# One 512-column matmul for both halves of the activations in 81 weight-stationary projections

## The chip, the cores and the metric

The kernel runs on one core of one Trainium2 chip. The metric is the time of one execution on the device in microseconds (us). Of the engines, TensorE (PE; PEld is its loading of weights) multiplies, VectorE (DVE) and ScalarE (ACT) work on elements, GpSimd (POOL) does small work, and SyncE (SP) starts the transfers of the weights.

## The reference

Two blocks of two layers each run on one sequence of 256 tokens with 1024 features, in float32.

```python
def first_block(...):
    for i in range(DEPTH):                      # 2
        h = h + mixer(rmsnorm(h, norm_mix[i]))  # 0: retention, 1: band attention
        h = h + ffn(rmsnorm(h, norm_ffn[i]))    # 0: SwiGLU of 2816, 1: 8 experts, top 2
        h = h + per_layer_embedding(...)
    return rmsnorm(h, norm_final)

def second_block(x, ...):
    for l in range(DEPTH):                      # 2
        h = rms_norm(x, norm_mix[l])
        x = x + hybrid_mixer(h, ...)            # stick-breaking, top-k attention, HGRN2
        h2 = rms_norm(x, norm_mlp[l])
        x = x + jnp.square(jax.nn.relu(h2 @ w_up[l])) @ w_down[l]
    return x
```

Each `@` with a weight is one of the projections below. The SwiGLU's gate and up weights, the MLP's up weights, the queries and keys of retention and of attention, and the `hq`, `hf`, `sq`, `sk` columns of `w_in` are those that the change touches.

## The kernel before

Every product with a weight is made of three matmuls (`mm3`, L337): both operands are split into a high part and a low part (`whi`, `wlo` for weights, `xth`, `xtl` for activations), and hi*hi, hi*lo and lo*hi are added in one PSUM bank of 128 partitions x 512 float32. The weights come from HBM in chunks (`wraw`) and are split in the kernel, `whi` on ACT (L288) and `wlo` on DVE (L289), into 5 buffers that run ahead of PE. So PE, ACT and DVE all work on every weight, and each engine does its instructions in the order in which a scheduler wrote them down when the kernel was built.

There are two kinds of projection. In `lin_tok` (and `down`) the activations are the stationary operand and the weights pass as 512 columns. In `lin_feat` (L422) it is the other way: the stationary is a 128x128 piece of weights and the 256 tokens pass, so its output has features on the partitions and tokens along the row. A call of `lin_feat` makes 256 features in two halves `f`, each with 8 steps `k` over the 1024 features of the input, three matmuls of 256 columns per step. Both halves go to one bank, side by side, and the caller reads the 512 columns straight from PSUM with its own first operation (L580 and L582 in retention, L707 in the dense layer, L793 in attention, L1356 and L1358 for the stick-breaking keys, L1421 and L1431 for HGRN2, L1524 in the MLP).

`lin_feat` is called 81 times: 8 in retention, 21 in the dense layer, 8 in attention, and in each of the two layers of the second block 4 for HGRN2, 3 for stick-breaking and 15 in the MLP. The banks that it takes turns through (`banks(mm=...)`) are three in the dense layer and the MLP ("012") and two elsewhere ("01" or "45").

In the MLP each step j makes one `lin_feat` and then the `down` product of step j-1: 24 matmuls of 512 columns that add up in four banks of their own (`acc`). Between the two stand the square of the rectified projection (L1524, L1525) and its split (`hh`, `hl`). In the hybrid layer PE gets the `lin_feat` matmuls of stick-breaking while DVE is busy with `select_keys` (L1310 to L1318), which finds the 64 best keys of each query.

## Time and profile before

| | |
|---|---|
| time, median of 3 runs | 2466.2 us (2464.65 to 2468.09) |
| the profiled execution | 2464.32 us |
| its span, first to last instruction | 2462.5 us |
| granted TensorE clock, mean | 0.997 |

The profiled execution is one more run of the same program, and the rows below are from it. Its time stands 1.9 us under the median, and 1.8 us of it lie around the span.

### The profile page before, as it was taken

What the parts mean: (1) busy time and instruction counts of PE and PEld (TensorE: products, weight loads), DVE (VectorE), ACT (ScalarE), POOL (GpSimd) and SP (SyncE); (2) the same over time, 40 slices, a digit from 0 to 9 for tenths busy, and PEclk for the clock granted to TensorE, in tenths of its full rate; (3) what the DMA queues carried; (4) which work ended last, traced back from release to release, by engine and by line L of the source; (5) the groups of instructions that cost most, each with busy time, mean ns of one, the idle gap of its engine ahead of it and who ended that gap; (6) DMA issues with size and microseconds to landing.
All of it is one profiled execution on the core that took longest, in us unless ns stands there. A gap on an engine that the chain in (4) does not pass through costs nothing. (4 is left out here: it accounts for less than half of the span.)

```text
span 2462.5 us, 35589 instructions
## 1 busy us (share of the span) xinstructions
PE 2402.0 (98%) x13060; PEld 1987.3 (81%) x13060; DVE 1880.3 (76%) x2964; ACT 1564.7 (64%) x2607; POOL 61.3 (2%) x105
## 2 busy tenths in 40 slices
PE   8999999999999999998999999899999999999999
PEld 6978998887876787865788875698779989877998
DVE  6757557658989889888989899878676567867655
ACT  6446556657887777777777788645745554575554
POOL 0000000000000000000000000101000000100000
PEclk9999999999999999999999999999999999999999
DMA  7445555557989998999899989534255554434553
GB/s 283 171 165 215 190 187 187 192 234 279 368 319 393 346 370 338 362 351 352 336 366 353 362 349 378 152 130 172 105 177 209 188 173 133 172 113 173 192 193 111
DMA packets 88391, 605.70 MB, mean 246 GB/s; under 512 B 10480, under 2 KB 12144, under 8 KB 17296
## 3 DMA queue, kind: packets, MB, share of 16 engines
q1 hardware_dynamic: 85792, 593.91, 65.0%
q0 software_dynamic: 2416, 9.44, 1.7%
q8 instruction: 104, 1.70, 0.3%
q14 instruction: 79, 0.65, 0.1%
HBM read 602.26 MB, written 1.05 MB: 245 GB/s over the span
## 5 line engine op out<-in xcount | busy, mean ns | idle before, releaser
L289 DVE TENSOR_TENSOR wlo<-wraw,whi 128x512 fp32r<-128x512 f32 (+1 forms) x1656 | 1379.9, 875 | 366.9 <-ACT whi L288 355.2
L288 ACT ACTIVATE whi<-wraw 128x512 fp32r<-128x512 f32 (+1 forms) x1656 | 1201.6, 775 | 436.7 <-PE mm L340 203.6
L341 PE MATMUL mm<-xth,wlo 128*128 128x256 f32 x1296 | 363.5, 280 | 1.5 <-DVE wlo L289 1.5
L339 PE MATMUL mm<-xth,whi 128*128 128x256 f32 x1296 | 364.9, 282 | 0.0
L340 PE MATMUL mm<-xtl,whi 128*128 128x256 f32 x1296 | 364.3, 281 | 0.0
L341 PEld LDWEIGHTS mm<-xth,wlo 128*128 128x128 f32 x1296 | 246.7, 190 | 2.4 <-DVE wlo L289 1.7
L341 PE MATMUL acc<-whi,hl 128*128 128x512 f32 x624 | 247.1, 397 | 0.4 <-DVE hl L345 0.4
L340 PEld LDWEIGHTS mm<-xtl,whi 128*128 128x128 f32 x1296 | 243.7, 188 | 4.0 <-issue 2.5
L339 PEld LDWEIGHTS mm<-xth,whi 128*128 128x128 f32 x1296 | 243.6, 188 | 2.7 <-issue 1.1
L340 PE MATMUL acc<-wlo,hh 128*128 128x512 f32 x624 | 245.0, 393 | 0.0
L339 PE MATMUL acc<-whi,hh 128*128 128x512 f32 x624 | 231.7, 391 | 0.0
L340 PE MATMUL mm<-wlo,xth 128*128 128x512 f32 (+2 forms) x592 | 231.7, 392 | 0.0
L339 PE MATMUL mm<-whi,xth 128*128 128x512 f32 (+2 forms) x592 | 230.8, 390 | 0.4 <-ACT xth L344 0.3
L341 PE MATMUL mm<-whi,xtl 128*128 128x512 f32 (+2 forms) x592 | 229.3, 388 | 0.6 <-DVE xtl L345 0.6
L340 PE MATMUL mm<-wlo,xgh 128*128 128x512 f32 x560 | 222.8, 398 | 1.6 <-DVE wlo L289 1.6
L339 PE MATMUL mm<-whi,xgh 128*128 128x512 f32 x560 | 221.6, 396 | 0.0
L341 PE MATMUL mm<-whi,xgl 128*128 128x512 f32 x560 | 221.4, 395 | 0.0
L994 PE MATMUL mm<-wlo,xgh 128*128 128x512 f32 x336 | 148.3, 441 | 20.2 <-DVE wlo L289 17.5
L341 PEld LDWEIGHTS acc<-whi,hl 128*128 128x128 f32 x624 | 117.2, 188 | 24.0 <-DVE hl L345 1.7
L339 PEld LDWEIGHTS acc<-whi,hh 128*128 128x128 f32 x624 | 117.3, 188 | 23.5 <-ACT hh L344 0.8
L340 PEld LDWEIGHTS acc<-wlo,hh 128*128 128x128 f32 x624 | 117.4, 188 | 21.2 <-DVE wlo L289 0.3
L993 PE MATMUL mm<-whi,xgh 128*128 128x512 f32 x336 | 133.0, 400 | 1.5 <-ACT whi L288 0.2
(410 smaller groups left out, 3169.6 us busy)
## 6 DMA issues: line engine op xcount, KB each, us to landing
wraw<-in_we_dram SPq DMA_DIRECT2D x336, 1024.0 KB, 6.0
wraw<-in_w_dram SPq DMA_DIRECT2D x218, 1024.0 KB, 4.8
wraw<-in_w_dram SPq DMA_DIRECT2D x4, 912.0 KB, 4.7
wraw<-in_w_dram SPq DMA_DIRECT2D x6, 512.0 KB, 3.6
bias<-in_rel_rows_dram POOLq DMA_DIRECT2D x4, 768.0 KB, 4.6
gain<-in_norm_ffn_dram POOLq DMA_DIRECT2D x2, 512.0 KB, 6.6
gn<-in_ret_gn_dram SPq DMA_DIRECT2D x4, 256.0 KB, 3.3
gain<-in_norm_ple_dram POOLq DMA_DIRECT2D x2, 512.0 KB, 5.4
```

Of the source, the lines that this page charges most:

```text
L288: self.nc.scalar.activation(h, src, AF.Copy)
L289: self.nc.vector.tensor_tensor(l, src, h.bitcast(F32), op=ALU.subtract)
L339: mm(out, l[0], r[0], start=start, stop=False)
L340: mm(out, l[0], r[1], start=False, stop=False)
L341: mm(out, l[1], r[0], start=False, stop=stop)
L993: nc.tensor.matmul(out, x[0], wk[0], start=start, stop=False)
L994: nc.tensor.matmul(out, x[0], wk[1], start=False, stop=stop)
```

## The change

`xT_tiles` makes one tile with both parts, `Parts.both` of [128, 2, 8, 256], whose two halves are used as `xth` and `xtl` were. For each half `f` and step `k`, `lin_feat` now passes hi and lo of the activations together, as 512 columns, by the high part of the weights, and the high part alone, as 256 columns, by the low part of the weights. The products with the hi columns and with the lo columns stand in two halves of a bank, so each `f` takes a bank of its own. On the way out ACT copies the lo half to SBUF and DVE adds the hi half to it; the callers then read the sum from SBUF. In the MLP the rectifying and squaring become one DVE instruction instead of an ACT and a DVE one.

```diff
--- before.py
+++ after.py
@@ -306,6 +306,14 @@
         return [[x[:, k, :] for x in self.hl[i]] for i in range(at, end) for k in range(self.parts[i][2])]
 
 
+class Parts(list):
+
+
+    def __init__(self, both):
+        super().__init__([both[:, 0], both[:, 1]])
+        self.both = both
+
+
 class Program:
     RAW, HL = 4, 5
 
@@ -381,7 +389,8 @@
             self.split_psum(dst[0][:, k0:k0 + n, b * P:(b + 1) * P], dst[1][:, k0:k0 + n, b * P:(b + 1) * P], t3)
 
     def xT_tiles(self, pool=None):
-        return [(pool or self.xt).tile([P, KD, T], F32R, name=n) for n in ("xth", "xtl")]
+        both = (pool or self.xt).tile([P, 2, KD, T], F32R, name="xt")
+        return Parts(both)
 
     def turned_h(self, gain, out, by_half=False):
 
@@ -419,14 +428,19 @@
                 self.mm3(ps[:, :n], [x[:, k, b * P:(b + 1) * P] for x in xT], w, k == 0, k == len(rows) - 1)
             use(b, ps[:, :n])
 
-    def lin_feat(self, xT, key):
+    def lin_feat(self, xT, key, out):
 
         w = self.w.get(key)
-        ps = self.bank("mm").rearrange("p (f t) -> p f t", t=T)
+        mm = self.nc.tensor.matmul
         for f in range(2):
+            ps = self.bank("mm").rearrange("p (i t) -> p i t", t=T)
             for k in range(KD):
-                self.mm3(ps[:, f, :], [x[:, f * P:(f + 1) * P] for x in w[k]], [x[:, k, :] for x in xT], k == 0, k == KD - 1)
-        return ps
+                hi, lo = (a[:, f * P:(f + 1) * P] for a in w[k])
+                mm(ps, hi, xT.both[:, :, k, :], start=k == 0, stop=False)
+                mm(ps[:, 0], lo, xT[0][:, k, :], start=False, stop=k == KD - 1)
+            self.nc.scalar.activation(out[:, f], ps[:, 1], AF.Copy)
+            self.nc.vector.tensor_tensor(out[:, f], out[:, f], ps[:, 0], op=ALU.add)
+        return out
 
     def table(self, name=None):
 
@@ -575,11 +589,11 @@
             on = {}
 
             def rotated(key):
-                ps = self.lin_feat(xT, key)
+                o = pool.tile([P, 2, T], F32, name=key[0] + "T", bufs=2)
+                self.lin_feat(xT, key, o)
                 a = pool.tile([P, 2, T], F32, name="rota", bufs=2)
-                nc.vector.tensor_tensor(a, ps, s2, op=ALU.mult)
-                o = pool.tile([P, 2, T], F32, name=key[0] + "T", bufs=2)
-                nc.vector.tensor_tensor(o, ps, c2, op=ALU.mult)
+                nc.vector.tensor_tensor(a, o, s2, op=ALU.mult)
+                nc.vector.tensor_tensor(o, o, c2, op=ALU.mult)
                 for f in range(2):
                     nc.vector.tensor_tensor(o[:, f, :], o[:, f, :], a[:, 1 - f, :], op=ALU.add)
                 return o
@@ -695,7 +709,7 @@
                             self.transposed([a[:, 0:1] for a in hT[0]], sg[:, 1], b, 1)
                         self.lin_tok(xT, [("du", 0)], 256, use)
                         continue
-                    ps = self.lin_feat(xT, ("du", j))
+                    gu = self.lin_feat(xT, ("du", j), pool.tile([P, 2, T], F32, name="gu"))
                     if j == 1:
                         row = self.row_of(self.plep, r)
                         with self.banks(mm="45", tp="67"):
@@ -703,8 +717,7 @@
                             for b in range(NB):
                                 for n in range(2):
                                     quarter(b, n)
-                    gu = pool.tile([P, 2, T], F32, name="gu")
-                    nc.vector.tensor_tensor(gu, ps, row[:, None, :].to_broadcast([P, 2, T]), op=ALU.mult)
+                    nc.vector.tensor_tensor(gu, gu, row[:, None, :].to_broadcast([P, 2, T]), op=ALU.mult)
                     sg = pool.tile([P, T], F32, name="sg")
                     nc.scalar.activation(sg, gu[:, 0, :], AF.Silu)
                     nc.vector.tensor_tensor(sg, sg, gu[:, 1, :], op=ALU.mult)
@@ -788,9 +801,8 @@
 
             def project(g):
                 for key, x in (("bk", xkv), ("bq", xq)):
-                    ps = self.lin_feat(x, (key, g))
-                    t = pool.tile([P, 2, T], F32, name=key, bufs=3)
-                    nc.vector.tensor_tensor(t, ps, row[:, None, :].to_broadcast([P, 2, T]), op=ALU.mult)
+                    t = self.lin_feat(x, (key, g), pool.tile([P, 2, T], F32, name=key, bufs=3))
+                    nc.vector.tensor_tensor(t, t, row[:, None, :].to_broadcast([P, 2, T]), op=ALU.mult)
                     kq[key, g] = t
 
             def attend(g):
@@ -1349,7 +1361,7 @@
         q = pool.tile([P, 3, T], F32, name="sq")
         k = pool.tile([P, 3, T], F32, name="sk")
         for i in range(3):
-            ps = self.lin_feat(self.x2, (("sq", i), l))
+            ps = self.lin_feat(self.x2, (("sq", i), l), self.work.tile([P, 2, T], F32, name="sqk", tag="xs", bufs=3))
             for f in range(2):
                 j = 2 * i + f
                 if j < 3:
@@ -1416,9 +1428,9 @@
         row = self.row_of(mix, r)
         rows = row[:, None, :].to_broadcast([P, 2, T])
         for i in range(2):
-            ps = self.lin_feat(self.x2, (("hf", i), l))
             sl = slice(2 * i, 2 * i + 2)
-            nc.vector.tensor_tensor(f[:, sl], ps, rows, op=ALU.mult)
+            self.lin_feat(self.x2, (("hf", i), l), f[:, sl])
+            nc.vector.tensor_tensor(f[:, sl], f[:, sl], rows, op=ALU.mult)
             self.in_table(nc.scalar.activation(f[:, sl], f[:, sl], AF.Sigmoid))
             if l:
                 for h in (2 * i, 2 * i + 1):
@@ -1426,11 +1438,11 @@
             nc.vector.tensor_scalar(k[:, sl], f[:, sl], -1.0, 1.0, op0=ALU.mult, op1=ALU.add)
             nc.vector.tensor_scalar(f[:, sl], f[:, sl], 1e-12, None, op0=ALU.max)
         for i in range(2):
-            ps = self.lin_feat(self.x2, (("hq", i), l))
+            qs = self.lin_feat(self.x2, (("hq", i), l), q[:, 2 * i:2 * i + 2])
             s = self.work.tile([P, 2, T], F32, name="sig", tag="xs", bufs=3)
-            nc.vector.tensor_tensor(q[:, 2 * i:2 * i + 2], ps, rows, op=ALU.mult)
-            self.in_table(nc.scalar.activation(s, q[:, 2 * i:2 * i + 2], AF.Sigmoid))
-            nc.vector.tensor_tensor(q[:, 2 * i:2 * i + 2], q[:, 2 * i:2 * i + 2], s, op=ALU.mult)
+            nc.vector.tensor_tensor(qs, qs, rows, op=ALU.mult)
+            self.in_table(nc.scalar.activation(s, qs, AF.Sigmoid))
+            nc.vector.tensor_tensor(qs, qs, s, op=ALU.mult)
         return (f, q, k, hv, og), row
 
     def hgrn(self, pool, st, levels):
@@ -1519,10 +1531,8 @@
                             self.transposed(hT[0], r, b, 2)
                         self.lin_tok(xT, [("mu", l, 0)], 256, use)
                         continue
-                    ps = self.lin_feat(xT, ("mu", l, j))
-                    r = pool.tile([P, 2, T], F32, name="r")
-                    nc.scalar.activation(r, ps, AF.Relu)
-                    nc.vector.tensor_tensor(r, r, r, op=ALU.mult)
+                    r = self.lin_feat(xT, ("mu", l, j), pool.tile([P, 2, T], F32, name="r"))
+                    nc.vector.scalar_tensor_tensor(r, r, 0.0, r, op0=ALU.max, op1=ALU.mult)
                     self.split_psum(*hT[j], r)
                     if j < nj - 1:
                         acc = acc or self.accumulators()
```

(The core of it, with all callers.) The scheduler writes the order of each engine anew. On PE, the end of an up-projection in the MLP of the last layer read like this before; `mm` is the projection's bank and `acc` those of `down`:

```order
L339 MATMUL mm<-xth,whi 128x256
L340 MATMUL mm<-xtl,whi 128x256
L341 MATMUL mm<-xth,wlo 128x256
L339 MATMUL mm<-xth,whi 128x256
L340 MATMUL mm<-xtl,whi 128x256
L341 MATMUL mm<-xth,wlo 128x256
L339 MATMUL acc<-whi,hh 128x512
```

And in the changed kernel, at the same place:

```order
L439 MATMUL mm<-xt,whi 128x512
L440 MATMUL mm<-xt,wlo 128x256
L439 MATMUL mm<-xt,whi 128x512
L440 MATMUL mm<-xt,wlo 128x256
L347 MATMUL acc<-whi,hh 128x512
```

Two steps `k` are now four matmuls instead of six, with the same 1536 columns in all.

On DVE, in the first hybrid layer, the first stick-breaking projection is read (L1356) among the instructions of `select_keys` (MAX and MATCH_REPLACE) and the splits of weights:

```order
L1317 MAX m_25449<-sc 128x8
L289 TENSOR_TENSOR wlo<-wraw,whi 128x512
L1318 MATCH_REPLACE sc_25447<-m_25449,sc 128x128
L289 TENSOR_TENSOR wlo<-wraw,whi 128x512
L1317 MAX m_25452<-sc_25447 128x8
L1356 SCALAR_TENSOR_TENSOR sq<-mm,rrow 128x256
L1318 MATCH_REPLACE sc<-m_25452,sc_25447 128x128
L1356 SCALAR_TENSOR_TENSOR sq<-mm,rrow 128x256
```

In the changed kernel the additions (L442) stand there, each for a bank of its own, and L1368, which was L1356, follows:

```order
L1329 MAX m_24990<-sc 128x8
L289 TENSOR_TENSOR wlo<-wraw,whi 128x512
L1330 MATCH_REPLACE sc_24988<-m_24990,sc 128x128
L289 TENSOR_TENSOR wlo<-wraw,whi 128x512
L1329 MAX m_24993<-sc_24988 128x8
L442 TENSOR_TENSOR sqk<-sqk,mm 128x256
L1330 MATCH_REPLACE sc<-m_24993,sc_24988 128x128
L442 TENSOR_TENSOR sqk<-sqk,mm 128x256
L1329 MAX m_24996<-sc 128x8
L1368 SCALAR_TENSOR_TENSOR sq<-sqk,rrow 128x256
```

The first addition stands where the first read of the bank stood, behind the same five instructions. On PE, four transposes of `rtq` that came after all three stick-breaking projections now come after the first.

Still on DVE, at the first HGRN2 projection of the second hybrid layer (`f`), the order before was:

```order
L289 TENSOR_TENSOR wlo<-wraw,whi 128x512 x6
L1412 SCALAR_TENSOR_TENSOR og<-mm,r,og 128x256
L1414 TENSOR_TENSOR og<-og,onorm 128x256
L289 TENSOR_TENSOR wlo<-wraw,whi 128x512 x4
L1421 TENSOR_TENSOR f<-mm,rrow 128x512
```

And in the changed kernel:

```order
L1426 TENSOR_TENSOR og<-og,onorm 128x256
L289 TENSOR_TENSOR wlo<-wraw,whi 128x512 x2
L442 TENSOR_TENSOR f<-f,mm 128x256
L289 TENSOR_TENSOR wlo<-wraw,whi 128x512 x3
L442 TENSOR_TENSOR f<-f,mm 128x256
L289 TENSOR_TENSOR wlo<-wraw,whi 128x512
L1433 TENSOR_TENSOR f<-f,rrow 128x512
```

The first half is taken out of its bank behind two splits, the second behind three more.

## Rows read from the trace of the kernel before

**Rows 1.** The page, busy time of each engine (share of the span) and instructions.
```profile
PE 2402.0 (98%) x13060; PEld 1987.3 (81%) x13060; DVE 1880.3 (76%) x2964; ACT 1564.7 (64%) x2607; POOL 61.3 (2%) x105
```

**Rows 2.** Stretches: length, each engine's busy us (instructions), clock, DMA share, GB/s.
```profile
243.00:398.00 155.00, 155.00 (x1100) 145.83 (x1100) 94.30 (x169) 79.04 (x148) 0.00 (x0) 1.00 0.54 190
...
1682.00:1705.00 23.00, 22.45 (x184) 20.58 (x184) 21.30 (x69) 12.34 (x25) 1.92 (x2) 1.00 0.46 155
...
1860.00:2015.00 155.00, 155.00 (x1008) 141.94 (x1007) 90.22 (x140) 79.82 (x140) 0.00 (x0) 1.00 0.56 191
```

**Rows 3.** Waits of PE: for whom, us in total, times, longest.
```profile
PE mm L994 <- DVE wlo L289: 17.5, 43, 0.8
...
PE mm L341 <- DVE wlo L289: 1.5, 1, 1.5
```

**Rows 4.** Groups by line on PE: count, busy us, mean ns, idle before.
```profile
L340 PE MATMUL mm<-xtl,whi 128*128 128x256 f32 x1296 | 364.3, 281 | 0.0
```

**Rows 5.** The same for PE's weight loads.
```profile
L340 PEld LDWEIGHTS mm<-xtl,whi 128*128 128x128 f32 x1296 | 243.7, 188 | 4.0 <-issue 2.5
```

**Rows 6.** Timeline of PE, one MLP step: start us, length us, instruction.
```profile
2297.44 0.28 PE L339 MATMUL mm<-xth,whi 128*128 128x256 f32 x1
...
2302.98 0.28 PE L341 MATMUL mm<-xth,wlo 128*128 128x256 f32 x1
2303.10 0.39 PE L339 MATMUL acc<-whi,hh 128*128 128x512 f32 x1
...
2308.54 0.28 PE L339 MATMUL mm<-xth,whi 128*128 128x256 f32 x1
```

**Rows 7.** Timeline of PE, second HGRN2 projection of the first hybrid layer.
```profile
1613.66 0.28 PE L341 MATMUL mm<-xth,wlo 128*128 128x256 f32 x1
...
1619.21 0.28 PE L339 MATMUL mm<-xth,whi 128*128 128x256 f32 x1
```

**Rows 8.** Timeline of PE, output product of the first hybrid layer.
```profile
1824.20 0.39 PE L339 MATMUL acc<-whi,xth 128*128 128x512 f32 x1
...
1831.20 0.39 PE L339 MATMUL acc<-whi,xth 128*128 128x512 f32 x1
```

**Rows 9.** Groups by line on DVE, shapes apart.
```profile
L345 DVE TENSOR_TENSOR hl<-tp,hh 128x256 fp32r<-128x256 f32 x74 | 31.0, 418 | 1.1 <-ACT hh L344 1.0
```

**Rows 10.** Groups by line on ACT, shapes apart.
```profile
L344 ACT ACTIVATE hh<-tp 128x256 fp32r<-128x256 f32 x74 | 28.3, 382 | 11.2 <-PE tp L1020 9.4 <-PE tp L379 1.5
...
L1524 ACT ACTIVATE r<-mm 128x512 f32<-128x512 f32 x30 | 17.5, 584 | 0.3 <-PE mm L341 0.3
```

**Rows 11.** Timeline of ACT behind the projection of rows 6.
```profile
2303.77 0.59 ACT L1524 ACTIVATE r<-mm 128x512 f32<-128x512 f32 x1
```

**Rows 12.** Timeline of PE, end of the first key projection of retention.
```profile
69.71 0.28 PE L341 MATMUL mm<-xth,wlo 128*128 128x256 f32 x1
```

**Rows 13.** Timeline of DVE behind it.
```profile
70.42 0.68 DVE L580 TENSOR_TENSOR rota<-mm,s 128x512 f32<-128x512 f32 x1
```

**Rows 14.** Timeline of PE, end of the first stick-breaking projection, first hybrid layer.
```profile
1693.08 0.28 PE L341 MATMUL mm<-xth,wlo 128*128 128x256 f32 x1
```

**Rows 15.** Timeline of DVE there: reads of the first and of the second projection.
```profile
1696.16 0.40 DVE L1356 SCALAR_TENSOR_TENSOR sq<-mm,rrow 128x256 f32<-128x256 f32 x1
...
1697.07 0.28 DVE L1317 MAX8 m<-sc 128x8 f32<-128x128 f32 x1
...
1702.63 0.41 DVE L1356 SCALAR_TENSOR_TENSOR sq<-mm,rrow 128x256 f32<-128x256 f32 x1
```

**Rows 16.** Timeline of PE, end of the first HGRN2 projection, second hybrid layer.
```profile
2045.90 0.28 PE L341 MATMUL mm<-xth,wlo 128*128 128x256 f32 x1
```

**Rows 17.** Timeline of DVE there.
```profile
2045.77 2.49 DVE L289 TENSOR_TENSOR wlo<-wraw,whi 128x512 fp32r<-128x512 f32 x4
2048.18 0.68 DVE L1421 TENSOR_TENSOR f<-mm,rrow 128x512 f32<-128x512 f32 x1
```

**Rows 18.** Timeline of PE, last product of the first MLP.
```profile
2017.05 0.39 PE L341 MATMUL acc<-whi,hl 128*128 128x512 f32 x1
2017.36 0.50 PE L339 MATMUL acc<-whi,hh 128*128 128x512 f32 x1
```

## The prediction

> **What bounds the kernel now.** The page's table of busy time comes first: TensorE is busy 98% of the span [rows 1]. Since matmuls overlap in that table, I asked next where PE truly waits. Among its waits there is one place worth 17.5 us, in the experts, which the change does not touch, and little else [rows 3]. The stretches say the same: in the dense layer and in the MLP, PE is busy in all of 155 us, DVE in 90 to 94 and ACT in about 80 [rows 2]. So the time is the number of matmuls times the distance from one start to the next, and a gain can only come from that distance. The exception to look for is a stretch where DVE is nearly full: while the stick-breaking projections run, DVE is busy 21.3 of 23 us [rows 2].
>
> So I read distances in the timeline, because a matmul's listed length of 281 ns [rows 4] is its whole way through the pipeline. In the MLP 48 matmuls of 256 columns start within 2303.10 - 2297.44 = 5.66 us, 117.9 ns each, and the 24 of 512 columns behind them within 5.44 us, 226.7 ns each [rows 6]. Elsewhere the same instructions go at another pace: in HGRN2 49 starts take 5.55 us, 113.3 ns each [rows 7], and 30 matmuls of 512 columns with the activations stationary take 7.00 us, 233.3 ns each [rows 8]. At 113.3 and 226.7 the cost goes by columns alone, with nothing per matmul.
>
> **The change part by part.**
>
> *PE.* 1296 steps (81 calls, 2 halves, 8 k) go from three matmuls of 256 columns to one of 512 and one of 256. The columns are the same 768; 1296 matmuls with their weight loads go. Where a step now takes 3 x 117.9 = 353.7 ns, I take the new pair at 226.7 + 117.9 = 344.6 ns, since just these two stand beside each other in the MLP: a saving of 9.1 ns a step, 146 ns a call. The dense layer and the MLP (51 calls) I count at this pace: 51 x 146 ns = 7.4 us saved. The other 30 calls I count at 3 x 113.3 = 339.9 ns a step, and there a pair of 344.6 loses 4.7 ns a step, 2.3 us in all. Together **-5.1 us**. The trace has no stream in which 512 and 256 alternate, so both ends stay open: a pair at 226.7 + 113.3 = 340 ns gives -11.2 us (13.7 x 816 steps, and nothing on the other 480), a pair at 233.3 + 117.9 = 351.2 gives -2.0 + 5.4 = +3.4 us.
>
> Here the Trainium skill has a rule to weigh. The trace shows a distance that doubles with the columns, 113.3 to 226.7 [rows 6, 7]. "TensorE: Matmul & The Clock Gate", section "Back-to-back issue gap", gives an isolated warm matmul N/2.4 + 2.5 ns, so a fixed 2.5 ns each. By it the 1296 matmuls would save 3.2 us, an estimate from that page, in place of the 5.1.
>
> *What the way out costs.* Each half now needs a copy of 256 columns from PSUM on ACT (382 ns for the like [rows 10]) and an addition on DVE (418 ns [rows 9]): 0.76 us on ACT and 0.84 us on DVE a call, 68 us of DVE work over 81 calls. Beside 11.1 us of PE work per MLP step that is covered: DVE has 40% of that stretch free [rows 2]. If the cover went, it would be 0.84 us a call. The first reading of the bank starts 0.79 us after the last matmul's start in the MLP [rows 6, 11] and 0.71 us in retention [rows 12, 13], so in such places the copy and the addition, some 1.6 us together, end well before the half bank is wanted again, which with two banks is 2.7 us later (16 matmuls, 8 pairs of 340 to 345 ns). In dense and MLP there are three banks and more room still.
>
> *Stick-breaking.* Here the room is missing. The first projection's last matmul starts at 1693.08 [rows 14], but DVE, full with `select_keys`, reads it only at 1696.16, 3.1 us late, and the second read ends about 1697.1 [rows 15]. Before, the next projection took the other bank and PE never noticed. Now the two halves fill both banks, and the third half needs the first one emptied. The addition stands in DVE's row where the first read stood, so the bank comes free at 1696.16 + 0.42 = 1696.58. PE could start at about 1693.2, and has only four small transposes to put in between, under 0.5 us. PE waits from 1693.6 to 1696.6: 3.0 us. Behind that matmul all of PE waits, since its order is fixed. For the next bank, the order puts fewer splits between (four where there were six), and DVE reaches the second projection's addition about when PE wants it; I take nothing, with 1.5 us as the other end. The same happens in the second hybrid layer, so **+6.0 us**, with ends of 2 (DVE is less late) and 9.
>
> *HGRN2 in the second hybrid layer.* DVE is behind here too: the first projection's last matmul starts at 2045.90 [rows 16] and DVE reads it at 2048.18, after four splits in 2.41 us, 0.6 each [rows 17]. The new order puts the first addition behind two of them, at 2045.77 + 1.2 = 2046.97, done 0.42 later at 2047.4. PE wants that bank at 2046.0: **+1.4 us** (0 to 2.5). In the first layer the trace has no such lag.
>
> *Ends of the stages.* The chain behind a last projection grows by copy and addition less the rectifying: 0.382 + 0.418 - 0.584 = 0.22 us [rows 9, 10]. At the end of the first MLP PE already gets there as `hh` and `hl` come: its step is 0.31 us where 0.23 is usual [rows 18]. So 0.2 us there, and as much for the ends of the dense layer and the second MLP together: **+0.4 us** (0 to 1.5).
>
> The sum is -5.1 + 6.0 + 1.4 + 0.4 = **+2.7 us** on the profiled execution's 2464.3, that is 2467.0; that execution lies 1.9 us under the median of the runs, so against the median of 2466.2 I say **2469 us**.
>
> **The rivals.** For all, less than 0.2% (4.9 us) is about what a measurement of this kernel can't tell from no change.
>
> *The waits do not reach the end (faster).* Place: the two stick-breaking stretches and HGRN2. If DVE, no longer given as many splits ahead, has emptied the bank when PE comes, then 7.4 us of waits go and the pace stays: -5.1 + 0.4 = -4.7, near 2461, and 2455 with the 340 ns pair. It decides from a lag of under 0.5 us where the trace has 3.1. For it: the order of both engines is new. Against: the lag is DVE's own work, 21.3 of 23 us [rows 2], and the change adds 0.84 us a call to it.
>
> *The pair runs slowly (slower).* A 512 that always costs 233.3 and a 256 that costs 117.9 give +3.4 in place of -5.1: +11.2 us, near 2477; with 9 us for stick-breaking 2480. It decides where a pair costs more than 346 ns (1296 pairs then save under 2.9 us, and the sum passes +4.9). For it: both paces stand in the trace, and which of them a stream gets seems to hang on what ran before it. Against: the MLP's `down` streams, next to the projections, all have the fast pace of 512.
>
> *Loads of weights in series.* If a load did not overlap the matmul before it, each of the 1296 that go would give back its 188 ns [rows 5], 244 us, near 2222 us. Against it: one load and one matmul together take 117.9 ns, less than the load's own length. "TensorE: Matmul & The Clock Gate", section "Part 3: Packing small matmuls — row/col tiling", says that loads overlap matmuls in flight only in other row groups, which would make this one true; the trace disagrees.
>
> *No change in the stream at all.* If the distance goes by columns, as 113.3 to 226.7 says, PE gives 0, and the waits stay: +7.8 us, near 2474.
>
> **How the numbers follow.** The forecast (pace gain and waits nearly cancel) 0.42. Waits not felt 0.20, of which most falls beyond -4.9 only together with a pair under 344 ns. Slow pair 0.20. No gain in the stream 0.17. Loads in series 0.01. Splitting each at 4.9 us: faster 0.20, within 0.42, slower 0.38. The range takes the fast pair without waits at its lower end and the slow pair with the longer waits at its upper: 2456 to 2481. The forecast's own range is 2464 to 2473.
>
> **What would show it.** In the MLP, starts of 512 and 256 should alternate with some 345 ns a pair, and a step of 11.10 us [rows 6] should become 10.95. In the stick-breaking stretch PE's first 512-column matmul of the second projection should wait about 3 us for DVE, in both layers, and once 1.4 us in the second layer's HGRN2. DVE should gain 68 us of busy time with no effect elsewhere. I am wrong if the pair's distance is under 341 or over 349, if these waits are absent, or if PE waits for banks in retention or attention, where I count nothing.

## The result, and the profile after

| | before | changed |
|---|---|---|
| median of 4 runs | 2467.05 us (2464.65 to 2468.09) | 2489.28 us (2485.78 to 2490.42) |
| the profiled execution | 2464.32 us | 2490.42 us |
| its span | 2462.5 us | 2488.7 us |
| granted TensorE clock, mean | 0.997 | 0.994 |

The ratio is 1.0092, with a 95% interval of 1.008 to 1.0104. The change costs 22.2 us where the forecast said +2.7, and 2489 lies outside the range of 2456 to 2481. The two profiled executions lie 26.1 us apart, more than the medians, since that of before is 2.7 us under the median here and that of the changed kernel 1.1 above. What single stages differ by in the two traces is a part of the 26.1.

The page, against [rows 1]: 1296 matmuls fewer, as counted, but PE is busy longer. DVE gained 66.4 us of work, where the prediction had 68.

```profile
PE 2417.6 (97%) x11764; PEld 1936.7 (78%) x11764; DVE 1946.7 (78%) x3126; ACT 1600.1 (64%) x2739; POOL 62.3 (3%) x105
```

The pace comes first, as it was the largest term. This is PE's timeline over one MLP step, against [rows 6]:

```profile
2323.06 0.39 PE L439 MATMUL mm<-xt,whi 128*128 128x512 f32 x1
2323.29 0.28 PE L440 MATMUL mm<-xt,wlo 128*128 128x256 f32 x1
...
2325.53 0.40 PE L439 MATMUL mm<-xt,whi 128*128 128x512 f32 x1
2325.76 0.28 PE L440 MATMUL mm<-xt,wlo 128*128 128x256 f32 x1
2325.88 0.40 PE L439 MATMUL mm<-xt,whi 128*128 128x512 f32 x1
...
2328.71 0.39 PE L347 MATMUL acc<-whi,hh 128*128 128x512 f32 x1
...
2334.18 0.39 PE L439 MATMUL mm<-xt,whi 128*128 128x512 f32 x1
```

Sixteen pairs take 2328.71 - 2323.06 = 5.65 us, 353.1 ns each: 0.23 us behind a 512, 0.12 behind a 256. Before, the same columns took 5.66 us as three matmuls. The 24 matmuls of `down` behind them keep their 227 to 228 ns. So the step stays at 11.12 us (11.10 before; forecast 10.95). In the first stick-breaking projection the timeline has the same pace:

```profile
1701.11 0.40 PE L439 MATMUL mm<-xt,whi 128*128 128x512 f32 x1
...
1704.64 0.40 PE L439 MATMUL mm<-xt,whi 128*128 128x512 f32 x1
```

Ten pairs in 3.53 us are 353 ns. Outside the dense layer and the MLP three matmuls took 339.9 ns [rows 7], so such calls lose 13 ns a step.

The waits of PE that are new or longer, against [rows 3] (for whom, us in total, times, longest):

```profile
PE mm L439 <- DVE sqk L442: 5.1, 2, 2.7
...
PE mm L439 <- DVE og L1424: 2.7, 2, 2.0
...
PE sc L816 <- DVE s L755: 1.4, 4, 0.4
```

The first line is the stick-breaking wait, once in each layer (2.7 and 2.4 us). The second is HGRN2, 2.0 us in the second layer and 0.7 in the first, where the forecast saw no lag. The timeline of all engines shows it, against [rows 14, 15]:

```profile
1702.29 3.37 DVE L1322 SCALAR_TENSOR_TENSOR sc<-rel,iw,sc 128x128 f32<-128x128 f32 x10
1702.47 0.38 ACT L441 ACTIVATE sqk<-mm 128x256 f32<-128x256 f32 x1
...
1705.00 0.60 PE L1242 MATMUL tp<-ident,rtq 128*128 128x128 f32 x4
...
1706.19 0.67 DVE L289 TENSOR_TENSOR wlo<-wraw,whi 128x512 fp32r<-128x512 f32 x1
...
1707.85 0.40 DVE L442 TENSOR_TENSOR sqk<-sqk,mm 128x256 f32<-128x256 f32 x1
...
1708.30 0.53 PE L439 MATMUL mm<-xt,whi 128*128 128x512 f32 x1 [2.71 <-DVE sqk L442]
1708.64 0.41 PE L440 MATMUL mm<-xt,wlo 128*128 128x256 f32 x1
1708.85 0.63 PE L439 MATMUL mm<-xt,whi 128*128 128x512 f32 x1
1709.28 0.41 PE L440 MATMUL mm<-xt,wlo 128*128 128x256 f32 x1
1709.49 0.63 PE L439 MATMUL mm<-xt,whi 128*128 128x512 f32 x1
```

ACT copies its half at once. DVE comes to the addition only at 1707.85, behind scores, splits and `select_keys`, and PE goes on 2.71 us late. What no step of the forecast had stands in the last rows: behind the wait a pair takes 1709.49 - 1708.85 = 0.64 us. The windows say why (length, busy us of each engine, granted clock, DMA share, GB/s):

```profile
1694.00:1717.00 23.00, 19.97 (x109) 15.94 (x108) 20.32 (x67) 11.89 (x26) 1.92 (x2) 0.93 0.39 137
1708.00:1712.00 4.00, 3.70 (x12) 3.17 (x13) 4.00 (x16) 0.00 (x0) 0.00 (x0) 0.58 0.00 0
...
2064.00:2068.00 4.00, 4.00 (x16) 3.40 (x16) 2.34 (x5) 2.56 (x5) 0.00 (x0) 0.62 0.79 279
```

For most of 4 us the granted clock is at the lower of its two levels (1.2 of 2.4 GHz). Over the stretch of 23 us it is 0.93, where it was 1.00 [rows 2]: 7% of 23 is 1.6 us. The third window is the same thing behind the 2.0 us wait in HGRN2 of the second layer.

### The profile page after: what moved, and what is told of

Its sections match the earlier page's. It is cut to its first block, busy times and chain, and to the rows that moved or that the text cites. A ratio compares the mean times of both kernels' runs of the same rounds, so it can differ in the third digit from the quotient of the medians.

```text
span 2488.7 us, 33278 instructions
## 1 busy us (share of the span) xinstructions
PE 2417.6 (97%) x11764; PEld 1936.7 (78%) x11764; DVE 1946.7 (78%) x3126; ACT 1600.1 (64%) x2739; POOL 62.3 (3%) x105
## 5 line engine op out<-in xcount | busy, mean ns | idle before, releaser
L439 PE MATMUL mm<-xt,whi 128*128 128x512 f32 x1296 | 466.9, 401 | 7.8 <-DVE sqk L442 5.1
L440 PE MATMUL mm<-xt,wlo 128*128 128x256 f32 x1296 | 369.5, 285 | 0.2 <-DVE wlo L289 0.2
L439 PEld LDWEIGHTS mm<-xt,whi 128*128 128x128 f32 x1296 | 245.2, 189 | 69.1 <-DVE sqk L442 5.6
L440 PEld LDWEIGHTS mm<-xt,wlo 128*128 128x128 f32 x1296 | 244.9, 189 | 5.4 <-issue 2.5
L348 PE MATMUL mm<-wlo,xt 128*128 128x512 f32 (+2 forms) x592 | 231.7, 392 | 1.0 <-DVE wlo L289 1.0
L347 PE MATMUL acc<-whi,hh 128*128 128x512 f32 x624 | 232.2, 392 | 0.0
L347 PE MATMUL mm<-whi,xt 128*128 128x512 f32 (+2 forms) x592 | 231.4, 391 | 0.8 <-ACT whi L288 0.5
L349 PE MATMUL mm<-whi,xt 128*128 128x512 f32 (+2 forms) x592 | 229.7, 389 | 0.5 <-DVE xt L353 0.5
L347 PE MATMUL mm<-whi,xgh 128*128 128x512 f32 x560 | 222.0, 397 | 0.0
L347 PEld LDWEIGHTS acc<-whi,hh 128*128 128x128 f32 x624 | 117.3, 188 | 25.8 <-ACT hh L352 0.8
L349 PEld LDWEIGHTS mm<-whi,xt 128*128 128x128 f32 x592 | 112.4, 190 | 23.0 <-issue 1.9
L347 PEld LDWEIGHTS mm<-whi,xt 128*128 128x128 f32 x592 | 112.6, 190 | 21.7 <-ACT whi L288 1.0
```

Of the source, the lines that this page charges most:

```text
L347: mm(out, l[0], r[0], start=start, stop=False)
L348: mm(out, l[0], r[1], start=False, stop=False)
L349: mm(out, l[1], r[0], start=False, stop=stop)
L439: mm(ps, hi, xT.both[:, :, k, :], start=k == 0, stop=False)
L440: mm(ps[:, 0], lo, xT[0][:, k, :], start=False, stop=k == KD - 1)
```

## The experiments

The kernel before ran beside each of them, with medians of 2466.3 to 2467.2 us. The changed kernel is taken at 2489.3. Where both medians are of 4 or 5 executions, which lie 3 to 7 us apart, their difference is good to some 3 to 4 us.

**Why is a pair 353 ns?** First the layout: hi and lo of one `k` side by side, as one run of 512 columns.

```diff
-        both = (pool or self.xt).tile([P, 2, KD, T], F32R, name="xt")
+        both = (pool or self.xt).tile([P, KD, 2, T], F32R, name="xt")
...
-                mm(ps, hi, xT.both[:, :, k, :], start=k == 0, stop=False)
+                mm(ps, hi, xT.both[:, k], start=k == 0, stop=False)
```

> The activations' tile is laid out [128, 8, 2, 256] instead of [128, 2, 8, 256], so that the 512 columns of hi and lo lie in one run of SBUF instead of two runs 8 KB apart; all else is as in the changed kernel, where 512 then 256 columns go at 235 + 118 = 353 ns. Theory A (the two runs of the moving operand cost the extra 8 ns): the pair goes to 340 to 345 ns, 1296 x 8 to 13 ns = 10 to 17 us less than the changed kernel, 2472 to 2479 us. Rival B (the layout in SBUF has no part in it): the pair stays at 353 ns and the time at 2487 to 2491 us.

Measured: 2491.0 us (2489.84 to 2492.51). An MLP step takes 11.12 us as before. Rival B: the layout has no part in it.

Then the half of the bank that the low weights' product goes to:

```diff
-                mm(ps[:, 0], lo, xT[0][:, k, :], start=False, stop=k == KD - 1)
+                mm(ps[:, 1], lo, xT[0][:, k, :], start=False, stop=k == KD - 1)
```

> The changed kernel, but the product with the low part of the weights is added to the other half of the bank (the half of the lo columns); the sum is the same. So a 256-column matmul adds to the half that the 512 before it wrote last, and the next 512 begins in a half that no matmul just wrote. Theory R (the 512 that begins in the half just written has to wait for it): 256 to 512 falls from 118 to 113 ns and the pair to 345 ns or less, 8 to 13 us less than the changed kernel, 2476 to 2481 us. Rival S (the half has no part in it): 353 ns and 2487 to 2491 us.

Measured: 2491.94 us (2490.19 to 2494.52), the MLP step again 11.12 us. Rival S as to the pace; the time lies 1 us above what S said.

Then the order, all matmuls of 512 columns of a half first:

```diff
             for k in range(KD):
-                hi, lo = (a[:, f * P:(f + 1) * P] for a in w[k])
-                mm(ps, hi, xT.both[:, :, k, :], start=k == 0, stop=False)
-                mm(ps[:, 0], lo, xT[0][:, k, :], start=False, stop=k == KD - 1)
+                mm(ps, w[k][0][:, f * P:(f + 1) * P], xT.both[:, :, k, :], start=k == 0, stop=False)
+            for k in range(KD):
+                mm(ps[:, 0], w[k][1][:, f * P:(f + 1) * P], xT[0][:, k, :], start=False, stop=k == KD - 1)
```

> Per half, all eight matmuls of 512 columns first, then the eight of 256; the same instructions in another order. Theory C (a change of width from one matmul to the next is what costs, as rows of 512 alone go at 226.7 ns and rows of 256 alone at 113.3 or 117.9): 226.7 + 113.3 to 117.9 = 340 to 345 ns a step, 10 to 17 us less than the changed kernel, 2472 to 2479 us. Rival D (512 columns cost 233 to 235 ns wherever the weights are the stationary): still 351 to 353 ns a step and 2487 to 2491 us.

Measured: 2482.26 us (2480.5 to 2484.53), 7.0 less than the changed kernel: between C and D. PE's timeline of an MLP step shows that a part of theory C holds:

```profile
2325.41 2.03 PE L438 MATMUL mm<-xt,whi 128*128 128x512 f32 x8
2327.28 1.08 PE L440 MATMUL mm<-xt,wlo 128*128 128x256 f32 x8
2328.20 2.02 PE L438 MATMUL mm<-xt,whi 128*128 128x512 f32 x8
2330.06 1.07 PE L440 MATMUL mm<-xt,wlo 128*128 128x256 f32 x8
2330.97 0.39 PE L347 MATMUL acc<-whi,hh 128*128 128x512 f32 x1
```

Eight matmuls of 512 take 1.87 us, 234 ns each, even among their like. Those of 256 fall from 118 to 115 ns. A step is 5.56 / 16 = 347.5 ns, 5.6 less than 353.1, and 1296 steps make 7.3 us of that, about the gain.

The same grouping in the kernel before, with no wide matmul:

```diff
+        mm = self.nc.tensor.matmul
         for f in range(2):
             for k in range(KD):
-                self.mm3(ps[:, f, :], [x[:, f * P:(f + 1) * P] for x in w[k]], [x[:, k, :] for x in xT], k == 0, k == KD - 1)
+                for x in xT:
+                    mm(ps[:, f, :], w[k][0][:, f * P:(f + 1) * P], x[:, k, :], start=k == 0 and x is xT[0], stop=False)
+            for k in range(KD):
+                mm(ps[:, f, :], w[k][1][:, f * P:(f + 1) * P], xT[0][:, k, :], start=False, stop=k == KD - 1)
```

> The kernel before with one change: in each half of the projection the 16 matmuls by the high part of the weights come first (hi and lo of the activations in turn, as 256 columns each), then the 8 by the low part. No wide matmul, no second bank, no copy. Theory K (the order of the stationaries sets the pace: with the low parts grouped, 256 columns go at 113.3 to 114.5 ns also in the dense layer and the MLP, where they took 117.8): 816 steps x 10 to 13.5 ns = 8 to 11 us less than before, 2456 to 2459 us. Rival L (the gain of grouping in the changed kernel was only that 512 and 256 no longer alternate): no change, 2465 to 2469 us.

Measured: 2465.83 us, 0.9996 of before (0.9986 to 1.0005). Theory K falls, and the time is rival L's: in the MLP 48 matmuls still take 5.65 us.

**What does merging itself give?** All of the way out kept, but from the second `k` on two matmuls of 256 in place of the 512:

```diff
-                mm(ps, hi, xT.both[:, :, k, :], start=k == 0, stop=False)
+                if k:
+                    mm(ps[:, 0], hi, xT[0][:, k, :], start=False, stop=False)
+                    mm(ps[:, 1], hi, xT[1][:, k, :], start=False, stop=False)
+                else:
+                    mm(ps, hi, xT.both[:, :, k, :], start=True, stop=False)
```

> The halves, the banks, the copy and the addition stay as in the changed kernel, but from the second step k on the 512 columns go as two matmuls of 256, so 7 of 8 steps are three matmuls of 256 again. Theory E (merging gives PE nothing; the loss is all in what surrounds it: the later release of banks, the copies, and the clock behind the waits): the step is 340 to 354 ns, the waits of the changed kernel stay, and the time is 2474 to 2490 us, at least 7 us over the kernel before. Rival F (merging does save the 9 ns a step of my forecast and something else eats it): 1134 steps x 9.1 ns = 10 us more than the changed kernel, about 2499 us.

Measured: 2488.38 us (2486.12 to 2490.38), the time of the changed kernel. Theory E: 1134 matmuls more cost nothing that such runs can tell (rival F said 10 us), so the 1296 fewer gave nothing. In the first stick-breaking projection PE's timeline reads:

```profile
1701.47 0.28 PE L440 MATMUL mm<-xt,whi 128*128 128x256 f32 x1
...
1703.59 0.28 PE L440 MATMUL mm<-xt,whi 128*128 128x256 f32 x1
```

Six steps of three matmuls in 2.12 us are 353 ns each, as the pairs took there. So the 13 ns that such calls lose do not come with the wide matmul. The loss is in what surrounds it.

**Where is the loss?** The new projection in some callers only, the one of before (kept as `lin_feat3`) in the others, which read its bank themselves again. In attention, for one, that is:

```diff
-                    t = self.lin_feat(x, (key, g), pool.tile([P, 2, T], F32, name=key, bufs=3))
-                    nc.vector.tensor_tensor(t, t, row[:, None, :].to_broadcast([P, 2, T]), op=ALU.mult)
+                    ps = self.lin_feat3(x, (key, g))
+                    t = pool.tile([P, 2, T], F32, name=key, bufs=3)
+                    nc.vector.tensor_tensor(t, ps, row[:, None, :].to_broadcast([P, 2, T]), op=ALU.mult)
```

The new one in the dense layer and the MLP alone:

> The new projection only in the dense layer and in the MLP (51 calls of 81); retention, attention, stick-breaking and HGRN2 get the projection of the kernel before. Theory G (in these 51 calls a step took 353.7 ns before and 353 now, and three banks hide the way out; the loss stands in the other 30 calls): 2466 to 2471 us, +0 to +4 on the kernel before. Rival H (the loss goes with the number of calls): 51/81 of 22 us = +14, near 2481 us.

Measured: 2467.76 us, 1.0005 (0.9995 to 1.0014). Theory G: 51 calls of 81 cost 0.6 us, not to be told from nothing. The same with grouped matmuls:

> Wide matmuls, grouped (eight of 512, then eight of 256 columns, per half), in the dense layer and the MLP alone; the projection of the kernel before elsewhere. In the grouped run these stood at 232.6 + 114.4 = 347 ns a step against 353.7 before. Theory C (so it is free of the waits and keeps that gain): 816 x 6.7 ns = 5.5 us less than before, 2460 to 2464 us. Rival M (what the grouping gains in pace goes in waits for splits of weights, whose buffers come free later): 2466 to 2469 us.

Measured: 2465.68 us, 0.9995 (0.9985 to 1.0004), between what C and M said. It can't be told from the kernel before, so no version here beats it. In retention alone, and in attention alone:

> The new projection in retention alone (8 calls). With dense layer and MLP at +0.6 us, stick-breaking at 8.7 and HGRN2 at 2.6 by the runs so far, some 11 of the 22 us are left for retention and attention, where the profile of the changed kernel shows +1.1 and +3.4 us. Theory N (retention costs what its stage shows): +1 to +2 us, 2467 to 2470 us. Rival O (the rest of the 11 us starts here): 2471 us or more.

> The new projection in attention alone (8 calls). Theory N (attention costs what its stage shows): +3 to +4 us, 2469 to 2471 us; the rest of the 11 us is then in the stretch behind the experts, which none of these edits touches and which swings between runs. Rival P (what attention delays is paid again behind it, at the experts and at the norm ahead of the hybrid layer): +6 to +10 us, 2473 to 2477 us.

Measured: retention 2466.69 us, 1.0004 (0.9995 to 1.0013), not to be told from nothing and 0.3 us under what theory N said; rival O falls. Attention 2470.67 us, 1.0016 (1.0007 to 1.0025), +3.8 us: theory N. From the last `down` of the dense layer to attention's last output product PE's timeline runs from 404.93 to 557.07 in this run, 152.14 us, and from 405.13 to 553.89 in the kernel before, 148.76.

The other way round: stick-breaking alone back to the old projection,

```diff
-            ps = self.lin_feat(self.x2, (("sq", i), l), self.work.tile([P, 2, T], F32, name="sqk", tag="xs", bufs=3))
+            ps = self.lin_feat3(self.x2, (("sq", i), l))
```

> The three stick-breaking projections of each hybrid layer alone get the projection of the kernel before (one bank for both halves, read by the caller); all else as in the changed kernel. Theory W (the late emptied banks cost): the waits of 2.9 and 2.6 us of PE go, with them the stretch at half clock behind the first (about 1.7 us), and 6 calls x 16 steps x 13 ns = 1.2 us of pace; 7 to 10 us less than the changed kernel, 2479 to 2482 us. Rival X (the wait is only a place: the selection of keys on DVE sets when the stage ends, and PE waits for it elsewhere): 2486 to 2490 us.

and HGRN2 besides:

> Stick-breaking and HGRN2 of both hybrid layers get the projection of the kernel before; retention, attention, dense layer and MLP keep the new one. Theory W: besides the 7 to 10 us of stick-breaking, the waits of 2.1 and 0.9 us in HGRN2 go, the stretch at half clock behind the longer one (1.7 us) and 8 x 16 x 13 ns = 1.7 us of pace, 5 to 7 us more: 2472 to 2477 us, of which 3 to 5 us over the kernel before are attention and 1 to 2 retention. Rival Y (the loss lies in retention and attention, and the hybrid layers only pass on what is late): 2481 us or more.

Measured: 2480.63 us (2478.82 to 2482.45) without stick-breaking, 8.7 less: theory W. The stretch is again as it was in [rows 2]:

```profile
1695.00:1718.00 23.00, 22.45 (x184) 20.34 (x182) 21.30 (x67) 12.29 (x25) 1.92 (x2) 1.00 0.43 147
```

And 2478.04 us (2474.85 to 2478.88) with HGRN2 back too: 2.6 less, half of what theory W said, with 11.8 us left over the kernel before. The difference is no larger than its noise; the two profiled executions lie 4.5 us apart.

**Is it the banks?** Four banks for the stick-breaking projections:

```diff
         for i in range(3):
-            ps = self.lin_feat(self.x2, (("sq", i), l), self.work.tile([P, 2, T], F32, name="sqk", tag="xs", bufs=3))
+            with self.banks(mm="4501" if i % 2 == 0 else "0145"):
+                ps = self.lin_feat(self.x2, (("sq", i), l), self.work.tile([P, 2, T], F32, name="sqk", tag="xs", bufs=3))
```

> The changed kernel, but the stick-breaking projections take turns through four banks (those of HGRN2's and stick-breaking's own products, idle then, besides the two), so that no half waits for the half two before it. Copy, addition and wide matmul stay. Theory W (it is the banks): the waits of 2.9 and 2.6 us and the stretch at half clock behind the first go, 6 to 8 us less than the changed kernel, 2481 to 2484 us. Rival Q (the additions themselves, six more instructions a layer on a DVE that is full there, make the stage longer): 2487 to 2490 us.

Measured: 2488.8 us (2486.35 to 2491.73). No gain: theory W fails, and the time is rival Q's. Its waits show that the wait has moved, to the gate's product (L347), which takes over the third projection's bank:

```profile
PE mm L347 <- DVE sqk L442: 4.6, 2, 2.4
```

So the gate was given other banks than the third projection:

```diff
-            with self.banks(mm="4501" if i % 2 == 0 else "0145"):
+            with self.banks(mm="45" if i % 2 else "01"):
```

> As the run with four banks, but the first and the third stick-breaking projection take the two banks of stick-breaking's own products and the second the two usual ones, so that the gate's product behind them gets banks that were read long before. Theory W (PE waits because a bank is wanted before DVE comes to its addition): no wait of 2 us for an addition is left, 6 to 8 us less than the changed kernel, 2481 to 2484 us. Rival T (the wait moves once more, to stick-breaking's own products, which need both the banks and the sums): 2486 to 2490 us.

Measured: 2487.51 us (2484.16 to 2490.12). No wait for an addition is left, as W said, but the time is T's. PE does not wait at the place that T named, but for DVE's next late thing, a split of weights:

```profile
1724.70 0.40 PE L347 MATMUL mm<-whi,xt 128*128 128x512 f32 x1
1727.08 0.50 PE L348 MATMUL mm<-wlo,xt 128*128 128x512 f32 x1 [1.98 <-DVE wlo L289]
```

Last, the banks of the changed kernel, but in stick-breaking ACT copies the hi half and nothing is added (the hi*lo part is left out there). `add` is False in stick-breaking alone:

```diff
-            self.nc.scalar.activation(out[:, f], ps[:, 1], AF.Copy)
-            self.nc.vector.tensor_tensor(out[:, f], out[:, f], ps[:, 0], op=ALU.add)
+            self.nc.scalar.activation(out[:, f], ps[:, int(add)], AF.Copy)
+            if add:
+                self.nc.vector.tensor_tensor(out[:, f], out[:, f], ps[:, 0], op=ALU.add)
```

> The changed kernel, but in stick-breaking alone the half of the lo columns is not added: ACT copies the hi half out and DVE does nothing for the bank, so the hi*lo part is left out of these three projections. Banks, wide matmuls and copies stay. Theory DVE (DVE, busy 28.3 of 30 us there, has no room for six additions of 0.42 us a layer, and they also stand late in its order): PE waits for no bank any more and not for splits, 6 to 9 us less than the changed kernel, 2480 to 2483 us, as with the old projection. Rival BANK (two banks for six halves cost by themselves, whoever empties them): PE still waits 2 us or more a layer there, 2485 to 2489 us.

Measured: 2483.08 us (2477.05 to 2483.94), 6.2 less than the changed kernel, and of PE's waits in the stretch only 0.2 us for ACT is left. The waits decide, and the time fits. Theory DVE: with two banks and six halves PE does not wait, once DVE has nothing to do for them.

**Do the costs add up?** Stick-breaking and attention both back to the old projection, by the two edits shown:

> The changed kernel with the projection of the kernel before in stick-breaking and in attention. By the runs so far: 2480.6 without stick-breaking, and attention alone is worth 3.8. Theory U (the costs add up): 2476 to 2478 us. Rival V (attention also causes the late load of weights and the longer stretch at half clock behind the experts, which cost the changed kernel some 3 us more than the runs with one part): 2471 to 2475 us, and PE's wait in front of the norm's transposes there falls from 3.4 us to 2 or less.

Measured: 2475.01 us (2474.13 to 2477.8). That is 5.6 under the run without stick-breaking, against 3.8 for attention alone, and at V's edge. V said that PE's wait behind the experts would be 2 us or less. The waits of PE and of ACT there:

```profile
PE tp L387 <- DVE xs L401: 3.0, 2, 2.4
...
ACT whi L288 <- DMA wraw<-in_w_dram: 2.5, 1, 2.5
```

So the longest is 2.4 us. Behind it the window shows a clock that stays at 1.00:

```profile
1588.00:1598.00 10.00, 7.72 (x37) 6.26 (x38) 8.61 (x14) 6.33 (x16) 1.42 (x2) 1.00 0.63 218
```

## Why the prediction was wrong

**The step that failed: the pair at 226.7 + 117.9 = 344.6 ns.** It measured 353. The price of the 512 was taken from `down`, the fastest stream in the trace, and `down` keeps it; the new stream got the other price that I had read, the 233.3 ns of [rows 8], among its like too (234). In the dense layer and the MLP a step went from 353.7 to 353.1 ns, 0.5 us in all in place of 7.4 saved; the run with these alone shows +0.6. In the other 30 calls, counted at a loss of 4.7 ns a step, it is 353 - 339.9 = 13.1 ns: 480 x 13.1 ns = 6.3 us, which the costs of the stages below contain. Together some +5.8 in place of -5.1, over half of the miss (1.7 us of it would be retention's, whose run shows no loss that can be told from nothing). My rival of the slow pair (351.2 ns) had the number, and "wrong if over 349" names it; for the dense layer and the MLP the rival of no change in the stream had it too. The reason that I gave the slow pair, a 512 that always costs 233.3, is not shown: three matmuls of 256 took the same 353 ns in such calls, and so did calls of the old projection (last section). What gives a stream its pace is open.

The rule that I weighed stands in the Trainium skill, "TensorE: Matmul & The Clock Gate", section "Back-to-back issue gap": by it each matmul less gives back 2.5 ns. The trace of the MLP has 0.6 ns a step, and 1134 matmuls put back cost nothing that the run shows.

**Stick-breaking: place and length right, price too low, reason half right.** PE waits 5.1 us in the two layers (forecast 6.0), at the second projection, for the addition. By the run that undid it, the part costs 8.7 us. To the waits come the lower clock behind the first, 1.6 us, and six calls at the slower pace, 6 x 16 x 13 ns = 1.2 us: 7.9 in sum. I blamed the bank. But with other banks the wait goes to the gate or to the splits, and without the additions it goes away with the old banks. DVE is full there, 21.3 of 23 us [rows 2], and six additions of 0.41 us are 2.4 us more in each layer. My sentence that the additions are covered by free DVE time was made for the MLP; the 0.84 us a call that it names for a cover that goes would have been 5.0 us for these six calls, near the 5.1 us that PE waits.

**HGRN2: 1.4 us forecast, 2.6 by the runs.** In the second layer the wait is 2.0 us, but for DVE's reading of an earlier bank (`og`, L1424), not for the addition: two halves now take both banks, and the second one meets the bank of the product ahead of it, which DVE reads behind six splits. The 1.5 us wait of [rows 3] at this place is gone in exchange. The clock near its lower level behind it was not counted, nor the 0.7 us that PE waits for `og` in the first layer.

**Attention: counted at nothing, measured +3.8.** "Wrong if PE waits in attention" holds in small: PE's wait for DVE in front of the scores grew from 0.6 us in 3 places to 1.4 in 4. The rest of the 3.4 us that the stage's trace is longer stands in no single wait; the pace (8 x 16 x 13.1 ns = 1.7 us at most) and another order of the small matmuls are in it, and I did not separate them. Retention, where I also counted nothing, shows no wait, and by its run no loss that can be told from nothing.

**Behind the experts: not in the forecast, and not settled.** The parts that the runs show make 0.6 + 3.8 + 2.6 + 8.7 = 15.7 us of 22.2; the other 6.5 us are in no experiment. In the trace part of them lies at the norm ahead of the hybrid layer, in instructions that the change leaves alone. There ACT waits for a weight to arrive, and all behind it in ACT's row, the norm's copy (L352) included, waits too. ACT's timeline in the changed kernel:

```profile
1592.10 0.63 ACT L288 ACTIVATE whi<-wraw 128x512 fp32r<-128x512 f32 x1 [3.29 <-DMA wraw<-in_w_dram]
1592.64 0.58 ACT L352 ACTIVATE xt<-tp 128x512 fp32r<-128x512 f32 x1
```

PE's wait that follows, and then the window behind it:

```profile
PE tp L387 <- DVE xs L401: 3.8, 2, 3.2
```

```profile
1596.00:1603.00 7.00, 6.94 (x25) 5.38 (x25) 4.98 (x9) 3.37 (x7) 0.21 (x1) 0.76 0.43 154
```

In the trace of before, PE waits 1.7 us there in all, and the clock stays at 1.00. From the last matmul ahead of the wait to the 18th product behind it PE takes 1601.88 - 1592.26 = 9.62 us, and 1591.98 - 1586.12 = 5.86 before, so 3.8 of the 26.1 us between the two traces arise here. My reading of [rows 3], 17.5 us in the experts and little else, passed this place over; over the whole trace of before the same view has

```profile
PE tp L379 <- DVE xs L392: 9.0, 4, 4.8
```

But that the change brings this is not shown. ACT's wait for that weight is 1.2 us before, 3.3 in the changed kernel, and in the run with the dense layer and the MLP alone:

```profile
ACT whi L288 <- DMA wraw<-in_w_dram: 3.2, 1, 3.2
```

With retention alone it is 2.7 us, with attention alone 1.9, and with grouped matmuls everywhere 0.3. Two of these runs can't be told from the kernel before by their time, and the long wait comes without the new projection in attention, so V's reason is not borne out. Why the load lands later is open.

**What held.** The DVE work added (66.4 us), its cover in the dense layer and the MLP and the ends of these stages, as far as their run (+0.6 us) can tell, and that the loads of weights do not set the pace.

## What to carry to other kernels

Where a trace shows one kind of matmul at two paces, a new stream is counted at the slower one until a run says more; here 2.4% of a distance turned PE's term from -5.1 to some +5.8 us. Fewer and wider matmuls with the same columns gained nothing here. An operation that is moved to another engine must be placed stage by stage: 0.4 us of DVE work cost nothing that shows in the MLP and about its full length where DVE was full, whatever bank it freed, and more where PE's wait also lowered the clock.

## What the runs showed of the hardware

The same matmuls run at two paces, within one call and from kernel to kernel. In the run with three matmuls a step, an MLP projection reads:

```profile
2322.42 0.39 PE L443 MATMUL mm<-xt,whi 128*128 128x512 f32 x1
...
2325.16 0.39 PE L443 MATMUL mm<-xt,whi 128*128 128x512 f32 x1
...
2327.97 0.39 PE L347 MATMUL acc<-whi,hh 128*128 128x512 f32 x1
```

The first half takes 2.74 us, 342.5 ns a step, the second, with the same instructions, 2.81 us, 351.3 ns. In the run with the new projection in the dense layer and the MLP alone, the second HGRN2 projection of the first hybrid layer, which is the old one as in [rows 7], reads:

```profile
1616.48 0.28 PE L347 MATMUL mm<-xt,whi 128*128 128x256 f32 x1
...
1622.13 0.28 PE L347 MATMUL mm<-xt,whi 128*128 128x256 f32 x1
```

These 48 matmuls take 5.65 us, 117.7 ns each, where [rows 7] has 113.3. The layout and the half of the bank had no part in the pace where they were tried, the order a small one; what sets it stays open.

Waits of PE of 2.7, 2.0 and 3.2 us were followed by a mean granted clock of 0.58, 0.62 and 0.76 over windows of 4, 4 and 7 us (above). The wait of 2.4 us at the second layer's stick-breaking projections was not, as the window behind it shows, nor was one of 2.4 us in the run without stick-breaking and attention:

```profile
2150.00:2154.00 4.00, 3.87 (x22) 3.37 (x23) 4.00 (x16) 0.39 (x1) 0.00 (x0) 1.00 0.00 0
```
